# A mixture-of-experts router's work behind the dense products, and its second square behind the copy of its transposes

## The chip, the cores and the metric

The kernel runs on one core of a Trainium2 chip. The metric is the device time of one execution in microseconds (us); lower is better. The core has five engines with a list of instructions each: TensorE (PE), VectorE (DVE), ScalarE (ACT), GpSimd (POOL) and SyncE (SP, which issues most of the transfers).

## The reference

Two transformer blocks for 512 tokens of width 1024, all in float32. The first has two attention branches and a dense MLP, the second a gated linear attention, a pooling branch and a mixture of experts. The change lies between the second block's attention and its experts:

```python
x = x + merged @ w_out[l]
h2 = rmsnorm_2(x, norm2_g[l])
x = x + hier_moe(h2, w_router_group[l], b_router_group[l], w_router_expert[l], b_router_expert[l],
                 w_exp_gate[l], w_exp_up[l], w_exp_down[l])
```

`hier_moe` computes 4 group logits and 32 expert logits for each token, takes the best group, in it the two best experts, sorts the assignments by expert and runs each expert on its tokens:

```python
g_logits = (ht @ w_rg) + b_rg
g_p, g_idx = lax.top_k(jax.nn.softmax(g_logits, axis=-1), 1)
e_all = jnp.einsum('td,gde->tge', ht, w_re) + b_re
e_logits = e_all[jnp.arange(T), g_idx[:, 0]]
e_top, e_idx = lax.top_k(e_logits, TOP_K_IN_GROUP)
```

## The kernel before

The 512 tokens are four tiles (`t` = 0 to 3) of 128 tokens on 128 partitions. Float32 products are made from float32r operands split into a high and a low part, with three products each (`three`, recorded at L605 like every product of this kind).

The order of the work is not written out: a planner (`Plan`, L422) holds a list of streams, generators that yield one operation at a time. It gives an operation the earliest start that its model allows and emits the one with the least key; the second number of `plan.go` is the stream's rank:

```python
key = (s + 40.0 * st[0], st[1])
```

So a stream of rank 20 is set back by 800 model nanoseconds against rank 0. PSUM banks (eight) and memory are handed out in the order of the ranks as well. What comes out is a fixed list for each engine. Each engine takes its own list in order, and waits on semaphores where an instruction needs another engine's result.

Around the change:

- `rows_out` (L1343) is the projection with `w_out`. For its second half of columns a dense unit of 24 products of 128x512 is made for each tile, and `s_addx` adds the result to the residual `X[t]` (DVE, L1339), which frees the unit's PSUM bank. It runs in the main stream, of rank 6.
- `s_h2(t)` (L1844) takes the squares of both halves of `X[t]` (ACT, L1852), the reciprocal root of their mean (`rstd`, L727: after the sum at L1855 seven short DVE operations, L737 to L747), scales the row (ACT, L1860) and writes it to memory as `hd` (SP, L1861).
- `s_router(t)` (L1864) does, for each half `a` of the columns, four PE transposes of `X[t]` into a bank (L1895), an ACT copy as the high part (L1898), a DVE subtraction as the low part (L1899) and 8 small products with the router's weights (L605, outputs of 72x128 and 36x128, for the last tile 128x72 and 128x36). For tiles 0 to 2 an ACT copy (L1907) and a product (L1910) then fold and turn the sums. At last DVE makes the logits (L1924; for the last tile L1921 and L1922).
- `route` (L1940) chooses groups and experts for the tiles in three cuts, tiles 0 and 1 together, then 2, then 3 (L1976 to L1991 and L1931), ranks the tokens (L1931, L2072, with small products on PE) and reads the row numbers out of PSUM (L2089, L2090). 14 products follow on PE whose result nobody uses (`s_warm`).
- The first gather (POOL, L2219) needs the row numbers and the four `hd` writes. The expert stage starts with the transposes of the gathered rows (L2276). The stream of expert weights (SP, L685) pauses from the end of the projection until the first gather has landed (`seen`, L669).

Of the kernel before, what the change touches and what calls it, by code (L numbers as in the profile page):

```python
# [22 lines left out]
NT = 4  # L23
# [516 lines left out]
def fused(ctx: ExitStack, tc: tile.TileContext, x_in, wd, we, sm, cst, out):  # L540
# [19 lines left out]
    plan = Plan()  # L560
# [8 lines left out]
    def act(fn, n, r, w, k=1):  # L569
        return ("act", 0.833 * n + 115.0 * k, fn, tuple(r), tuple(w))  # L570

    def dve(fn, n, r, w, k=1, fast=False):
        return ("dve", (0.52 if fast else 1.04) * n + 70.0 * k, fn, tuple(r), tuple(w))
# [15 lines left out]
    def give(*bufs, toks=()):  # L589
        for b in bufs:  # L590
            b.last = max([b.last] + [k.last for k in toks])
            b.mem.give(b)
# [56 lines left out]
    rt = {}  # L649
# [646 lines left out]
    def gates(hT, res, n=4, att=False, rows=None):  # L1296
        hi, lo, toks = hT_cols(hT)
        for c in range(n):
            i = next(wi)
            wh, wl = yield from weight(i)  # L1300
            for u in range(2):
                ps, = yield take(banks=1)
                yield from cols_unit(ps, wh, wl, KD, 256, u * P, hi, lo, toks)
                b, = yield spare(KEEP_GATE if att else 0, 512)
                res.append(b)
                plan.go(s_gate(ps, b, rows), 2)
            done_weight(i)
# [87 lines left out]
    def new_parts():  # L1395

        b = yield taker(*[KD // NB * S] * (2 * NB))
        h, l = ([q for c in bs for q in carve(c, KD // NB)] for bs in (b[:NB], b[NB:]))
        return list(zip(h, l)) + [b]
# [86 lines left out]
    def s_alpha():  # L1486
        w = yield from load_small("alpha")
        h, l = yield from split(w.f, 256, [w], high=True)
        give(w)
        alpha.extend((h, l))  # L1490
# [283 lines left out]
    def pool_units(hT, rows):  # L1774
        hi, lo, toks = hT_cols(hT)
        for c in range(2):
            i = next(wi)
            wh, wl = yield from weight(i)
            for u in range(2):
                ps, = yield take(banks=1)  # L1780
                yield from cols_unit(ps, wh, wl, KD, 256, u * P, hi, lo, toks)
                plan.go(s_pool(2 * c + u, ps, rows), 2)
            done_weight(i)
# [12 lines left out]
    def block2_body(hT, rows, x4):  # L1796
        if "late" not in cgot:
            yield ("wait", lambda: "late" in cgot)
        plan.go(s_alpha(), 5)
        plan.go(s_par(["b_alpha_2", "gla_norm_g_2", "pool_scale", "pool_w"]), 5)  # L1800
        yield from token_major(hT, W2_CHUNKS, SECT2, True)
        yield from pool_units(hT, rows)
        gp, gg = [], []
        yield from gates(hT, gp, rows=rows)
        if len(pooled) < 4:
            yield ("wait", lambda: len(pooled) == 4)
        ptoks = [b for g in range(4) for b in pooled[g]]
        yield from branch2(lambda k: pooled[k][0].r, lambda k: pooled[k][1].r, ptoks, gp)
        give(*ptoks)
        yield from gates(hT, gg, rows=rows)  # L1810
        give(*hT[0], *hT[1], toks=hT[2])
        if OT.get("g") is None:
            yield ("wait", lambda: OT.get("g") is not None)
        mg = yield from new_parts()
        split_ahead[0] = AHEAD_OUT2
        yield from branch(OT["g"], ottok["g"], gg, gp, mg)
        give(rows[1], *(fac[t][0] for t in range(NT)), toks=rows[0])
        plan.go(s_par(["router", "b_router"]), 4)
        if "b_router" not in par:
            yield ("wait", lambda: "b_router" in par)  # L1820
        w = par["router"]
        wv = w.f.rearrange("p (k n) -> p k n", k=KD)
        yield dve(lambda: tt(wv, wv, gain("norm2_g_2")[:, :, None].to_broadcast([P, KD, 36]), ALU.mult), 288,
                  [w, par["gains"]], [w])
        wr, = yield taker(576, high=True)
        wrv, wrf = (q.rearrange("p (k z n) -> p k z n", k=KD, z=2) for q in (wr.r, wr.f))
        wr.need = 2
        yield act(lambda: A.activation(wrv[:, :, 0], wv, AF.Copy), 288, [w], [wr])
        yield dve(lambda: tt(wrv[:, :, 1], wv, wrf[:, :, 0], ALU.subtract), 288, [w], [wr])
        rt["w"] = wr  # L1830
        give(w)
        rt["x4"] = x4
        for t in range(NT):
            plan.go(s_router(t, x4[t]), 0)
        plan.go(route(), 0)
        yield from rows_out(mg, x4, True, EXP_AHEAD)

# [6 lines left out]
    def s_h2(t, xtok):  # L1844

        ss, = yield take(small=[2])
        ss.need = 2
        j, = yield take(512)
        for n in range(2):
            if xtok[n].t is None:  # L1850
                yield ("wait", lambda: xtok[n].t is not None)
            yield act(lambda: A.activation(j.f, X[t][:, n * 512:(n + 1) * 512], AF.Square, accum_out=ss.f[:, n:n + 1]), 512,  # L1852
                      [xtok[n]], [ss, j], k=2)
        give(j)
        yield dve(lambda: V.tensor_tensor(ss.f[:, 0:1], ss.f[:, 0:1], ss.f[:, 1:2], op=ALU.add), 1, [ss], [ss])  # L1855
        rb, r = yield from rstd(ss.f[:, 0:1], 1, D, ss)
        give(ss)
        rt["r", t] = rb, r
        h, = yield take(D)
        yield act(lambda: A.activation(h.f, X[t], AF.Copy, scale=r), D, [*xtok, rb], [h])  # L1860
        yield dma(lambda: SP.dma_start(hd[t * P:(t + 1) * P, :], h.f), 4 * P * D, [h], [hdt[t]])  # L1861
        give(h)

    def s_router(t, xtok):  # L1864
# [23 lines left out]
        for a in range(2):  # L1888
            if xtok[a].t is None:
                yield ("wait", lambda: xtok[a].t is not None)  # L1890
            ps, = yield take(banks=1)

            def f():
                for k in range(4):
                    T.transpose(ps.f[:, k * P:(k + 1) * P], X[t][:, (4 * a + k) * P:(4 * a + k + 1) * P], C["ident"])  # L1895

            yield pe(f, 4 * 56, [xtok[a], cgot["ident"][0]], [ps])
            yield act(lambda: A.activation(hs[a].r, ps.f, AF.Copy), 512, [ps], [hs[a]])  # L1898
            yield dve(lambda: V.tensor_tensor(ls[a].r, ps.f, hs[a].f, op=ALU.subtract), 512, [ps, hs[a]], [ls[a]])  # L1899
            give(ps)  # L1900
            hv, lv = (q[a].r.rearrange("p (k s) -> p k s", k=4) for q in (hs, ls))
            yield pe(lambda: products(a), 8 * (60 if t < NT - 1 else 108), [wr, hs[a], ls[a]], [po])
# [27 lines left out]
    def tt(o, a, b, op):  # L1930
        V.tensor_tensor(o, a, b, op=op)  # L1931
# [692 lines left out]
    def s_par(names, mem=None):  # L2624
        for n in names:
            par[n] = yield from load_small(n, mem)
# [117 lines left out]
```

## Time and profile before

| | us |
|---|---|
| median of 3 runs | 1342.98 |
| lowest, highest | 1341.76, 1343.89 |
| the profiled execution, its own time | 1340.58 |
| its span, first to last instruction | 1338.8 |
| PE busy | 1302.4 |
| DVE busy | 795.6 |
| ACT busy | 510.2 |

A row of the timeline gives the start, the duration, the engine, the line, the operation, output <- input with the tile's name, and in brackets how long the engine was idle before and what released it. Rows of equal instructions that follow each other are merged, with their count. The chain of waits is followed back from the last instruction. The granted clock of PE is given as a share of 2.4 GHz. Times are from the start of the span.

### The profile page before, as it was taken

To read this page: it belongs to the slowest core of one execution; us is meant where nothing else is said; L and a number is where in the kernel's file an instruction comes from. 1 tells how busy PE (TensorE), PEld (TensorE's weight loads), DVE (VectorE), ACT (ScalarE), POOL (GpSimd) and SP (SyncE) were. 2 spreads that over 40 slices of the span, in tenths; PEclk is the share of its full clock that TensorE was granted. 3 is DMA by queue.
4 is the path that set the end of the run, shared out by engine and by line. 5 is a ranking of instruction groups with operands and counts; after the bars stand their busy time and mean duration, and the time that the engine had idled before them with its cause. 6 is when DMAs were issued, how large, how long until landed. Compare 5 with 4: busy or idle time off the path is not lost.

```text
span 1338.8 us, 18461 instructions
## 1 busy us (share of the span) xinstructions
PE 1302.4 (97%) x6917; PEld 1003.8 (75%) x6917; DVE 795.6 (59%) x1912; ACT 510.2 (38%) x1084; POOL 22.1 (2%) x31
## 2 busy tenths in 40 slices
PE   6999999999999999999999999999999899999995
PEld 6998987778888888888888998888887544544543
DVE  7789988937454434334347448953374437555556
ACT  6663475643354313223225555542333211122212
POOL 0000000000000000000000000000000100000000
PEclk9999999999999999999999999999999899999998
DMA  6212220134132322222232221122262599999992
GB/s 245 95 64 95 75 85 32 41 132 143 35 112 94 111 95 94 94 95 94 95 112 87 90 85 64 63 73 100 95 241 94 201 407 408 409 408 407 408 368 79
DMA packets 59214, 205.11 MB, mean 153 GB/s; under 512 B 8435, under 2 KB 8947, under 8 KB 59123
## 3 DMA queue, kind: packets, MB, share of 16 engines
q1 hardware_dynamic: 56738, 199.72, 40.8%
q0 software_dynamic: 2384, 4.20, 0.9%
q8 instruction: 55, 0.90, 0.3%
q14 instruction: 37, 0.29, 0.1%
HBM read 204.15 MB, written 4.19 MB: 156 GB/s over the span
## 4 chain that ended last, share of the span: by engine, by line
PE 93%; DVE 3%; DMA 3%; ACT 1%; issue 1%; SPq 0%; DVEq 0%; ACTq 0%; POOLq 0%
PE bank L605 88%; DMA b<-in_we_dram 2%; PE bank L1231 1%; PE bank L2276 1%; PE bank L775 1%; DMA b<-in_wd_dram 1%; PE bank L1007 0%; DVE b L2560 0%; DMA b<-hd,b 0%; DVE b L1339 0%; PE bank L2336 0%; PE bank L1031 0%; PE bank L1895 0%; ACT b L2552 0%; DVE b L1931 0%
## 5 line engine op out<-in xcount | busy, mean ns | idle before, releaser
L605 PE MATMUL bank<-b,b 128*128 128x512 f32 (+9 forms) x6271 | 1250.1, 387 | 8.5 <-DVE b L1931 4.5
L605 PEld LDWEIGHTS bank<-b,b 128*128 128x128 f32 (+1 forms) x6271 | 937.0, 181 | 278.1 <-issue 102.4
L711 DVE TENSOR_TENSOR b<-b,b 128x1024 fp32r<-128x1024 f32 (+4 forms) x160 | 193.3, 1225 | 86.1 <-ACT b L710 83.2
L710 ACT ACTIVATE b<-b 128x1024 fp32r<-128x1024 f32 (+4 forms) x160 | 167.8, 1059 | 175.8 <-PE bank L605 165.7
L1339 DVE TENSOR_TENSOR b<-bank,b 128x512 f32<-128x512 f32 x176 | 111.2, 684 | 83.4 <-PE bank L605 82.7
L2293 ACT ACTIVATE b<-bank 128x256 f32<-128x256 f32 x16 | 6.2, 385 | 147.4 <-PE bank L605 141.1
L1404 DVE SCALAR_TENSOR_TENSOR b<-bank,b 128x512 f32<-128x512 f32 x32 | 22.1, 692 | 67.1 <-PE bank L605 65.4
L1407 ACT ACTIVATE b<-b 128x512 f32<-128x512 f32 x32 | 20.2, 632 | 96.2 <-DVE b L1404 96.2
L2296 DVE SCALAR_TENSOR_TENSOR b<-b,bank 128x256 f32<-128x256 f32 x16 | 6.7, 422 | 81.4 <-ACT b L2293 81.4
L2360 DVE SCALAR_TENSOR_TENSOR b<-bank,b,b 128x512 fp32r<-128x512 f32 x34 | 25.5, 751 | 28.9 <-ACT b L2359 28.9
L2359 ACT ACTIVATE b<-bank,b 128x512 fp32r<-128x512 f32 x34 | 23.4, 688 | 41.4 <-PE bank L605 38.8
L1208 ACT ACTIVATE b<-b,smalls 128x256 f32<-128x256 f32 (+3 forms) x64 | 32.6, 512 | 12.7 <-DVE smalls L1195 12.7
L1410 DVE TENSOR_TENSOR b<-b,b 128x512 fp32r<-128x512 f32 x32 | 22.1, 689 | 21.8 <-ACT b L1409 21.8
L1290 DVE TENSOR_TENSOR b<-bank,b 128x512 f32<-128x512 f32 x16 | 11.1, 692 | 36.7 <-PE bank L605 36.6
L1310 DVE SCALAR_TENSOR_TENSOR b<-b,bank 128x512 f32<-128x512 f32 x32 | 21.9, 684 | 15.2 <-PE bank L605 15.0
L775 PE MATMUL bank<-b,b 128*128 128x128 f32 x96 | 16.3, 303 | 12.9 <-DVE b L890 12.9
L1185 DVE CUSTOM_DVE_ANT_0 b<-bank,b 128x256 f32<-128x256 f32 (+3 forms) x64 | 26.2, 432 | 1.3 <-PE bank L605 1.2
L1139 DVE MATCH_REPLACE8 b<-smalls,b 128x256 f32<-128x256 f32 (+2 forms) x48 | 26.0, 550 | 0.0
L1291 ACT ACTIVATE b<-b 128x512 f32<-128x512 f32 x16 | 10.1, 630 | 40.5 <-DVE b L1290 40.5
L1138 DVE MAX8 smalls<-b 128x8 f32<-128x256 f32 (+2 forms) x48 | 25.4, 557 | 0.0
L794 ACT ACTIVATE b<-b 128x1024 f32<-128x1024 f32 x16 | 17.0, 1064 | 21.9 <-DVE b L1339 13.2
L2276 PEld LDWEIGHTS bank<-b,b 128*128 128x128 f32 (+1 forms) x136 | 14.9, 145 | 13.0 <-DVE b L2360 8.9
(207 smaller groups left out, 811.3 us busy)
## 6 DMA issues: line engine op xcount, KB each, us to landing
b<-in_we_dram SPq DMA_DIRECT2D x198, 512.0 KB
b<-in_wd_dram SPq DMA_DIRECT2D x138, 512.0 KB
b<-in_wd_dram SPq DMA_DIRECT2D x8, 516.0 KB
b<-in_x_dram SPq DMA_DIRECT2D x8, 512.0 KB
b<-in_wd_dram SPq DMA_DIRECT2D x6, 544.0 KB
b<-in_wd_dram SPq DMA_DIRECT2D x4, 536.0 KB
b<-in_wd_dram SPq DMA_DIRECT2D x4, 520.0 KB
hd<-b SPq DMA_DIRECT2D x4, 512.0 KB
```

Source lines behind the costliest of these rows:

```text
L605: T.matmul(o, l, r, start=start, stop=stop, skip_group_check=True)
L710: yield act(lambda: A.activation(h.r, b.f, AF.Copy), m, [b], [h])
L711: yield dve(lambda: V.tensor_tensor(l.r, b.f, h.f, op=ALU.subtract), m, [b, h], [l])
L775: T.transpose(banks[a].f[:, k * P:(k + 1) * P], x[:, (4 * a + k) * P:(4 * a + k + 1) * P], C["ident"])
L1138: yield dve(lambda: V.max(m8.f, acc.f), nk, [acc], [m8])
L1139: yield dve(lambda: V.match_replace(out=acc.f, in_to_replace=m8.f, in_values=acc.f, imm_value=GONE), nk, [m8, acc], [acc])
L1185: yield dve(lambda: V.tensor_tensor_reduce(out=p[h].f, in0=ps.f[:, i * nk:(i + 1) * nk], in1=mask, scale=1.0, scalar=GONE, op0=ALU.add, op ...
L1208: yield act(lambda: A.activation(ph, ph, AF.Exp, bias=ng_[:, h:h + 1], scale=0.125, accum_out=sm_[:, h:h + 1]), nk, [p[h], st], [p[h], st] ...
L1339: yield dve(lambda: V.tensor_tensor(X[t][:, a:a + w], ps.f[:, :w], X[t][:, a:a + w], op=ALU.add), w, [ps, before or xt[t]], [tok])
L2276: T.transpose(ps.f[:, k * P:k * P + n], g.f[0:n, (4 * a + k) * P:(4 * a + k + 1) * P], C["ident"][0:n, 0:n])
L2359: yield act(lambda: A.activation(yh.r[:, s], ps.f, AF.Copy, scale=gt), 512, [ps, sg], [yh], k=2)
L2360: yield dve(lambda: V.scalar_tensor_tensor(yl.r[:, s], ps.f, gt, yh.f[:, s], op0=ALU.mult, op1=ALU.subtract), 512, [ps, sg], [yl])
```

## The change

The router's streams of tiles 0, 1 and 2 are given rank 20 instead of 0; that of tile 3 and `route` stay at 0. In `s_h2` a tile's second square is yielded only once the copy of that tile's second transposes has been recorded (`("turned", t)`).

```diff
@@ -1831,7 +1831,7 @@
         give(w)
         rt["x4"] = x4
         for t in range(NT):
-            plan.go(s_router(t, x4[t]), 0)
+            plan.go(s_router(t, x4[t]), 0 if t == NT - 1 else 20)
         plan.go(route(), 0)
         yield from rows_out(mg, x4, True, EXP_AHEAD)
 
@@ -1849,6 +1849,8 @@
         for n in range(2):
             if xtok[n].t is None:
                 yield ("wait", lambda: xtok[n].t is not None)
+            if n and ("turned", t) not in rt:
+                yield ("wait", lambda: ("turned", t) in rt)
             yield act(lambda: A.activation(j.f, X[t][:, n * 512:(n + 1) * 512], AF.Square, accum_out=ss.f[:, n:n + 1]), 512,
                       [xtok[n]], [ss, j], k=2)
         give(j)
@@ -1896,6 +1898,8 @@
 
             yield pe(f, 4 * 56, [xtok[a], cgot["ident"][0]], [ps])
             yield act(lambda: A.activation(hs[a].r, ps.f, AF.Copy), 512, [ps], [hs[a]])
+            if a:
+                rt["turned", t] = True
             yield dve(lambda: V.tensor_tensor(ls[a].r, ps.f, hs[a].f, op=ALU.subtract), 512, [ps, hs[a]], [ls[a]])
             give(ps)
             hv, lv = (q[a].r.rearrange("p (k s) -> p k s", k=4) for q in (hs, ls))
```

What becomes of it in the lists. On PE, at the end of tile 1's second unit of the projection; in these rows `bank` is a PSUM bank, `b_3368` the residual `X`, `b_85` the identity. Before:

```order
L605 MATMUL bank_68<-b_8859,b_8619 128x512
L1910 MATMUL bank_69<-b_3890,b_9073 128x36
L1895 MATMUL bank_68<-b_85,b_3368 128x128 x4
L1895 MATMUL bank_69<-b_85,b_3368 128x128 x4
L605 MATMUL bank_66<-b_8918,b_8803 72x128
```

With the change, at the same place:

```order
L605 MATMUL bank_68<-b_8859,b_8619 128x512
L1897 MATMUL bank_66<-b_85,b_3368 128x128 x4
L605 MATMUL bank_68<-b_8780,b_8612 128x512
L605 MATMUL bank_68<-b_8781,b_8612 128x512
L605 MATMUL bank_68<-b_8780,b_8616 128x512
```

The folds, transposes and small products of the router (which go on after the last row of before) are gone from here; a set of transposes stands between this unit and the next, which writes the same bank.

On ACT, the stretch around and after tile 3's residual add; `b_3368` is `X`, `smalls` holds sums and roots, and the buffer that a copy writes tells the tile: before, `b_9074` is the high part of tile 2 and `b_9111` that of tile 3; with the change `b_8918` is that of tile 1, `b_9114` of tile 2, `b_9107` of tile 3. Before, from tile 1's scaled row on:

```order
L1860 ACTIVATE b_9136<-b_3368,smalls 128x1024
L1898 ACTIVATE b_9111<-bank_66 128x512
L1852 ACTIVATE b_8943,smalls<-b_3368 128x512
L1898 ACTIVATE b_9074<-bank_69 128x512
L1907 ACTIVATE b_9221<-bank_65 72x128
L1860 ACTIVATE b_9234<-b_3368,smalls 128x1024
L1852 ACTIVATE b_8992,smalls<-b_3368 128x512
L1898 ACTIVATE b_9111<-bank_69 128x512
L1860 ACTIVATE b_9308<-b_3368,smalls 128x1024
```

With the change, from tile 0's scaled row on:

```order
L1862 ACTIVATE b_9109<-b_3368,smalls 128x1024
L1900 ACTIVATE b_9107<-bank_68 128x512
L1911 ACTIVATE b_9138<-bank_69 72x128
L1900 ACTIVATE b_9107<-bank_69 128x512
L1854 ACTIVATE b_8966,smalls<-b_3368 128x512
L1862 ACTIVATE b_9187<-b_3368,smalls 128x1024
L1900 ACTIVATE b_8918<-bank_69 128x512
L1854 ACTIVATE b_8920,smalls<-b_3368 128x512
L1900 ACTIVATE b_9114<-bank_66 128x512
```

The square (now L1854) stands behind the copy (now L1900) in each tile; tile 3's square and scaled row stand ahead of tile 1's second copy.

On DVE with the change, from tile 3's logits (L1925, L1926) to tile 1's (L1928); `b_8919` and `b_9115` are the low parts of tiles 1 and 2:

```order
L1925 SCALAR_TENSOR_TENSOR b_8806<-bank_66,smalls,b_8785 128x36
L1926 SCALAR_TENSOR_TENSOR b_8806<-bank_66,smalls,b_8806 128x36
L1857 TENSOR_TENSOR smalls<-smalls 128x1
L737 TENSOR_SCALAR smalls<-smalls 128x1
L738 TENSOR_SCALAR smalls<-smalls 128x1
L740 TENSOR_SCALAR smalls<-smalls 128x1
L744 SCALAR_TENSOR_TENSOR smalls<-smalls 128x1
L745 SCALAR_TENSOR_TENSOR smalls<-smalls 128x1
L746 SCALAR_TENSOR_TENSOR smalls<-smalls 128x1
L747 SCALAR_TENSOR_TENSOR smalls<-smalls 128x1
L1903 TENSOR_TENSOR b_8919<-bank_69,b_8918 128x512
L1903 TENSOR_TENSOR b_9115<-bank_66,b_9114 128x512
```

Before, this root and both subtractions stood ahead of tile 3's residual add; now tile 1's root stands ahead of tile 1's second subtraction, and all of it behind tile 3's logits.

## Rows read from the trace of the kernel before

**Rows 1.** Page, part 1: busy us, share of the span, instructions of PE.
```profile
PE 1302.4 (97%) x6917; PEld 1003.8 (75%) x6917; DVE 795.6 (59%) x1912; ACT 510.2 (38%) x1084; POOL 22.1 (2%) x31
```

**Rows 2.** Timeline of DVE, 1000 to 1068 us: start, us, engine, line, operation, tiles.
```profile
1040.46 0.25 DVE L1924 SCALAR_TENSOR_TENSOR b<-bank,smalls,b 128x36 f32<-128x36 f32 x1
...
1042.81 0.19 DVE L1931 TENSOR_TENSOR b<-b 128x32 fp32r<-128x32 f32 x1
...
1044.52 0.69 DVE L1339 TENSOR_TENSOR b<-bank,b 128x512 f32<-128x512 f32 x1 [1.52 <-PE bank L605]
...
1045.12 0.41 DVE L1931 TENSOR_TENSOR b<-b 128x32 f32<-128x32 f32 x2
...
1045.96 0.42 DVE L1931 TENSOR_TENSOR b<-b,b 128x256 fp32r<-128x256 f32 x1
...
1046.30 0.15 DVE L1855 TENSOR_TENSOR smalls<-smalls 128x1 f32<-128x1 f32 x1
...
1046.59 0.69 DVE L1899 TENSOR_TENSOR b<-bank,b 128x512 fp32r<-128x512 f32 x1
...
1048.14 0.16 DVE L747 SCALAR_TENSOR_TENSOR smalls<-smalls 128x1 f32<-128x1 f32 x1
...
1049.54 0.16 DVE L1976 TENSOR_REDUCE b<-b 128x1 f32<-128x4 f32 x1
...
1053.90 0.17 DVE L2089 TENSOR_SCALAR b<-bank 128x16 int32<-128x16 f32 x1 [0.69 <-PE bank L605]
```

**Rows 3.** Chain of waits, 1000 to 1250 us: start, us, what.
```profile
1054.95 4.35 DMA b<-hd,b
```

**Rows 4.** Timeline of PE, 1000 to 1062 us.
```profile
1005.87 0.60 PE L1895 MATMUL bank<-b,b 128*128 128x128 f32 x4
...
1006.22 3.50 PE L605 MATMUL bank<-b,b 128*128 128x512 f32 x20
...
1024.17 0.31 PE L1910 MATMUL bank<-b,b 72*128 72x36 f32 x2
...
1025.12 1.09 PE L1895 MATMUL bank<-b,b 128*128 128x128 f32 x8 [0.64 <-DVE b L1339]
...
1027.62 2.66 PE L605 MATMUL bank<-b,b 128*36 128x128 f32 x21 [0.45 <-DVE b L1899]
...
1047.33 1.58 PE L605 MATMUL bank<-b,b 128*128 128x36 f32 x7 [0.38 <-DVE smalls L738]
...
1053.26 5.78 PE L605 MATMUL bank<-b,b 128*128 128x16 f32 x16 [1.03 <-DVE b L1931]
```

**Rows 5.** Chain of waits, 1235 us to the end.
```profile
1238.27 14.15 PE bank L605 x64
...
1295.37 10.38 DMA b<-in_we_dram
...
1305.75 1.28 issue
```

**Rows 6.** Timeline of ACT, 1000 to 1068 us.
```profile
1032.18 1.15 ACT L1860 ACTIVATE b<-b,smalls 128x1024 f32<-128x1024 f32 x1 [2.58 <-DMA hd<-b]
...
1045.24 0.63 ACT L1852 ACTIVATE b<-b 128x512 f32<-128x512 f32 x1 [3.71 <-DVE b L1339]
...
1045.96 0.60 ACT L1898 ACTIVATE b<-bank 128x512 fp32r<-128x512 f32 x1
```

**Rows 7.** Stretches: length, busy us (instructions) by engine, granted clock, DMA share, GB/s.
```profile
1040.00:1053.20 13.20, 7.77 (x37) 6.32 (x37) 9.60 (x48) 3.61 (x5) 1.31 (x2) 0.78 0.44 159
...
1048.00:1050.00 2.00, 0.92 (x5) 0.80 (x4) 1.17 (x8) 1.15 (x1) 0.00 (x0) 0.50 0.00 0
...
1057.00:1058.00 1.00, 1.00 (x5) 0.76 (x4) 0.00 (x0) 0.00 (x0) 0.40 (x1) 0.64 0.65 201
```

**Rows 8.** Timeline of PE, 1230 us to the end.
```profile
1299.37 5.82 PE L605 MATMUL bank<-b,b 128*128 128x512 f32 x24
```

**Rows 9.** Stretches, the end of the expert stage.
```profile
1240.00:1300.00 60.00, 60.00 (x292) 27.94 (x291) 30.94 (x54) 11.70 (x31) 1.93 (x2) 1.00 1.03 404
```

## The prediction

> **What bounds the kernel now.** I read the page first, then the chain of waits, then the timelines of TensorE (PE), VectorE (DVE) and ScalarE (ACT) over the router, then the end of the chain. PE is busy for 1302.4 of 1338.8 us [rows 1], so only its idle stretches can be won or lost. The largest is the router's end: the last dense product of the output projection is followed by tile 3's residual add at 1044.52, the row numbers leave PSUM at 1053.90 [rows 2], and the expert stage cannot begin before the first gathered rows land, at 1054.95 + 4.35 = 1059.30 [rows 3]. In between PE has little but 14 filler products, in the row of 16 at 1053.26 [rows 4]. So there are two quantities: when the dense block ends (call it T, the start of tile 3's add; now 1044.52), and how long the tail from T to the row numbers is (now 1053.90 - 1044.52 = 9.4 us). The tail is that short because, before T, the routers of tiles 0 to 2 are nearly through: of 8 sets of transposes 7, of 8 groups of small products 7, and all three folds stand ahead of it on PE.
>
> **The change, part by part.** In the planner the three router streams lose to any dense unit that is ready. The order shows what that makes: the four dense units follow each other, and five sets of transposes, seven groups of small products, all three folds and all of the ranking move behind T.
>
> *The dense block gets shorter.* I count from 1005.87, the first transposes [rows 4], up to which both orders are the same. Still ahead of T are:
> - 114 dense products. 64 of them take 14.15 us [rows 5], 0.221 each: 25.2 us.
> - 3 sets of transposes, each 1006.22 - 1005.87 = 0.35 [rows 4]: 1.1 us.
> - one group of 8 small products. The row of 21 at 1027.62 holds 15 of them and 6 dense ones in 2.66 us [rows 4]: (2.66 - 6 x 0.221) / 15 = 0.09 each, so 0.7 us.
> - a new wait. The dense units of the four tiles now all use one PSUM bank, so each waits until DVE has added the one before. Where PE waits for such an add today, 1025.12 - 1024.17 = 0.95 us pass [rows 4]. At three places a set of transposes covers 0.35 of it, at one the small products cover 0.7: 3 x 0.6 + 0.25 = 2.05 us.
>
> Together 29.1 us; with 0.2 until the add starts, T is at 1035.2, which is **9.4 us earlier**.
>
> *The tail gets longer.* It is now a chain through what has moved there, in the order of the three lists; each link waits for the one before:
> 1. Tile 3's add, then its first transposes in that bank: 0.69 [rows 2] and 0.05 hand-over, 0.75.
> 2. PE: transposes 0.35, three groups of small products 24 x 0.09 = 2.2, the fold of tile 0 0.31 [rows 4], and its logits 0.25 [rows 2], whose reading frees the bank for tile 3's second transposes: 3.2.
> 3. Those transposes 0.60 [rows 4], the ACT copy 0.60, and now the second square, 0.72 before the next ACT start [rows 6]: 1.9.
> 4. Tile 3's reciprocal root on DVE, eight short operations from 1046.30 to 1048.14 + 0.16, less the 0.60 that a low-part subtraction takes among them [rows 2]: 1.4.
> 5. ACT: the scaled row copy 1.15, which waited for that root, then tile 1's copy and square behind it: 1.15 + 0.60 + 0.72 = 2.5 [rows 6].
> 6. Tile 1's root, which stands ahead of its low-part subtraction on DVE: 1.4 + 0.69 [rows 2] = 2.1.
> 7. PE: 7 + 8 small products, transposes, tile 1's fold. Warm: 15 x 0.09 + 0.35 + 0.31 = 2.0. Seven small products took 1.58 us, 0.2 each, where the granted clock was falling to 0.50 [rows 4, 7], the 1.2 GHz level. In the tail PE has by then been mostly waiting for some 8 us, so I take 0.2 each and twice the rest: 4.2.
> 8. DVE: logits and choice for tiles 0 and 1 with tile 2's root in between. For one tile 1040.46 to 1042.81 + 0.19 = 2.5 [rows 2]; two tiles have two more operations (0.4) and the root's eight fill gaps and add about 0.8 (an estimate from these rows): 3.7.
> 9. Tile 2's subtraction 0.60, ranks 1.3 (from 1045.12 to the end of the row at 1045.96 [rows 2]), its fold and the sums 0.6: 2.5.
> 10. Tile 2's choice and ranks: 2.5 + 1.3 = 3.8.
> 11. Tile 3's choice and ranks: 1049.54 to 1053.90 [rows 2] = 4.4.
>
> Sum 30.5 us against 9.4: **21.1 us more**. The row numbers come 21.1 - 9.4 = 11.7 later, at about 1065.6. The four row writes to memory, the last behind tile 2's root in link 8, have landed by then; the gather and its 4.35 us are as before.
>
> Of link 7 the Trainium skill (TensorE: Matmul & The Clock Gate, "Back-to-back issue gap") says that cold products start N / 1.2 GHz apart, 107 ns for 128 columns. By it the 15 products cost 1.6 us instead of 3.0 and the sum is 1.4 less; the trace has 0.2 us each for narrower ones, and that I use.
>
> *The second square behind the copy.* Today tile 3's square stands ahead of its copy, 1045.24 against 1045.96 [rows 6]; that 0.72 leaves the way to the last products. In link 3 the same square stands before the root that tile 1 waits for, so it is in the sum once and buys nothing.
>
> *The weight stream.* One expert weight load more (seven instead of six) is issued before the stream pauses for the gather. At the end the last load lands at 1305.75 and PE goes on 1.28 later [rows 5], while PE's own products were through at 1299.37 + 5.82 = 1305.19 [rows 8]. A load takes 10.38 / 8 = 1.3 us with eight in flight [rows 5], so the stream ends up to 1.3 earlier relative to the gather, of which 1305.75 - 1305.19 = 0.56 can be used: **-0.6**.
>
> Net +11.1 us. Against the profiled execution (1340.58) that is 1351.7; the median of the three runs is 2.4 above it, and I add the sum to the median: **1354.1 us**, slower by 0.8%. Bounds: with link 7 warm, nothing lost in link 8 and 1 us of overlap in links 2 and 9, it is 4 less, +7; with the small products of link 2 and the ranks' matmuls at half clock too (15 x 0.11 and some 0.3 a tile), and no use of the load, +14.
>
> **The rivals.**
> - *The tail overlaps (faster).* The chains of the three tiles are independent; if the engines ran them side by side, DVE's own work would set the tail. 83 DVE operations stand in it; 48 took 9.60 us in the router's second half [rows 7], so 0.2 each and 16.6 us. The net is -9.4 + 16.6 - 9.4 - 0.6 = -2.8: 1340.2. It decides at a tail of 19.4 us. Against it: each engine takes its list in order, and links 5 and 6 put one tile's wait ahead of another's work on ACT and on DVE. 0.04.
> - *PE stays at half clock into the expert stage.* Now the clock is back within the filler products, at 0.64 in 1057 to 1058 [rows 7], some 4 us after they start. If after the longer quiet it came 4 us later, expert products would run at half speed for as long and lose 2.1: 1356.2. The Trainium skill (the same page, "HAM oscillation") says that after an idle gap TensorE is re-throttled and pays again on every restart, which would favour this; the same 14 products stand before the gather in both orders, which speaks against. 0.08.
> - *The weight stream alone sets the end.* Then the seventh load is worth its full 1.3 us: 1353.4. For it: the DMA share is 1.03 from 1240 to 1300; against: PE is busy for 60.00 of the same 60 us [rows 9]. 0.08.
> - *The planner's order is not what the diff says*: excluded, since the order shows the units together and the copies ahead of the squares.
>
> **How the numbers follow.** The forecast as worked out has 0.80; all cases but the first rival are slower, and their times lie inside its bounds. The range is 1342.98 + 7 to 1342.98 + 14, 1350 to 1357; outside it I leave about 0.2, the first rival among it. About 0.2%, 2.7 us, is what a measurement can tell from no change: the first rival is split between faster and the same, so faster 0.02, same 0.03, slower 0.95.
>
> **What would show it.** Right: tile 3's add near 1035, the row numbers near 1065, a tail of 28 to 32 us in which DVE waits for ACT squares and PE waits for DVE subtractions, the granted clock at 0.50 from some 5 us after the add until the filler products, and from the gather on the same expert stage, shifted. Each of the four dense units should be followed by a wait of some 0.6 us for the add. Wrong: a tail under 20 us, or a dense block that does not end 8 to 10 us earlier, or an expert stage whose length changes by more than 2 us.

## The result, and the profile after

The changed kernel takes 1354.59 us (median of 4 runs, 1352.7 to 1355.02) beside 1343.09 for the kernel before on the same chip (4 runs, 1341.76 to 1343.89): 11.5 us more, a ratio of 1.0091 with a 95% interval of 1.0078 to 1.0104. Its profiled run took 1355.02 us. Lines from L1852 of the kernel before on stand 2 later than there, those from L1899 on 4 later.

The timeline of PE over the router, of the kernel after, answers to [rows 4]:

```profile
1023.67 5.80 PE L605 MATMUL bank<-b,b 128*128 128x512 f32 x24 [0.34 <-DVE b L1339]
1029.31 0.60 PE L1897 MATMUL bank<-b,b 128*128 128x128 f32 x4
1030.26 5.79 PE L605 MATMUL bank<-b,b 128*128 128x512 f32 x24 [0.35 <-DVE b L1339]
1036.83 0.66 PE L1897 MATMUL bank<-b,b 128*128 128x128 f32 x4 [0.79 <-DVE b L1339]
...
1038.90 0.95 PE L605 MATMUL bank<-b,b 128*128 128x36 f32 x7 [0.32 <-DVE b L1903]
...
1048.39 1.91 PE L605 MATMUL bank<-b,b 128*36 128x128 f32 x15 [2.36 <-DVE b L1903]
1050.10 1.06 PE L1897 MATMUL bank<-b,b 128*128 128x128 f32 x4
...
1054.94 3.26 PE L605 MATMUL bank<-b,b 128*128 128x64 f32 x18 [3.51 <-DVE b L1935]
...
1066.30 5.77 PE L605 MATMUL bank<-b,b 128*128 128x16 f32 x16 [1.03 <-DVE b L1935]
1072.87 1.06 PE L2280 MATMUL bank<-b,b 128*128 128x128 f32 x8 [0.80 <-DMA b<-hd,b]
```

The dense units stand together, 6.59 us apart, each behind a wait for the add that frees its bank. Then PE mostly waits until the filler products in the row at 1066.30 and the expert stage at 1072.87, which began at 1059.44 before.

DVE in the same stretch, beside [rows 2]:

```profile
1036.09 0.69 DVE L1339 TENSOR_TENSOR b<-bank,b 128x512 f32<-128x512 f32 x1 [2.80 <-PE bank L605]
...
1040.13 0.26 DVE L1928 SCALAR_TENSOR_TENSOR b<-bank,smalls,b 128x36 f32<-128x36 f32 x1 [1.29 <-PE bank L1914]
...
1042.38 0.16 DVE L1857 TENSOR_TENSOR smalls<-smalls 128x1 f32<-128x1 f32 x1
...
1046.24 0.16 DVE L1857 TENSOR_TENSOR smalls<-smalls 128x1 f32<-128x1 f32 x1 [1.71 <-ACT b L1854]
...
1047.65 1.28 DVE L1903 TENSOR_TENSOR b<-bank,b 128x512 fp32r<-128x512 f32 x2
1051.47 0.25 DVE L1928 SCALAR_TENSOR_TENSOR b<-bank,smalls,b 128x36 f32<-128x36 f32 x1 [2.53 <-PE bank L1914]
...
1058.71 0.26 DVE L1928 SCALAR_TENSOR_TENSOR b<-bank,smalls,b 128x36 f32<-128x36 f32 x1 [1.59 <-PE bank L1914]
...
1062.58 0.15 DVE L1980 TENSOR_REDUCE b<-b 128x1 f32<-128x4 f32 x1
...
1066.93 0.17 DVE L2093 TENSOR_SCALAR b<-bank 128x16 int32<-128x16 f32 x1 [0.69 <-PE bank L605]
```

Tile 3's add (T) is at 1036.09 instead of 1044.52, the row numbers leave at 1066.93 instead of 1053.90, and the tail between the two is 30.84 us instead of 9.38. The traces start up to 1.2 us apart, so I compare them from the first of these eight adds, which stands at 1001.99 before and at 1001.61 here: aligned there, T is 1036.47, 8.05 earlier, and the row numbers come at 1067.31, 13.4 later. ACT shows link 5 of the prediction: the scaled row of tile 3, then the copy and the square of tile 1, for whose root DVE waits until 1046.24.

```profile
1043.97 1.15 ACT L1862 ACTIVATE b<-b,smalls 128x1024 f32<-128x1024 f32 x1 [1.62 <-DVE smalls L747]
1045.02 0.58 ACT L1900 ACTIVATE b<-bank 128x512 fp32r<-128x512 f32 x1
1045.50 0.62 ACT L1854 ACTIVATE b<-b 128x512 f32<-128x512 f32 x1
```

The stretches (length, busy time of each engine with instructions, granted clock, DMA share, GB/s) beside [rows 7]: half clock from about 1043.4 on (0.93 in the first row), 7 us after the add, and full clock again at about 1070.7 (0.64 in the third), 4.4 us after the row of the fillers begins.

```profile
1040.00:1044.00 4.00, 2.54 (x17) 2.07 (x16) 2.17 (x11) 1.24 (x4) 0.00 (x0) 0.93 0.04 17
1044.00:1070.00 26.00, 13.89 (x63) 11.70 (x62) 14.94 (x78) 6.96 (x13) 1.71 (x2) 0.50 0.17 63
1070.00:1071.00 1.00, 1.00 (x5) 0.76 (x4) 0.00 (x0) 0.00 (x0) 0.43 (x1) 0.64 0.58 139
1071.00:1072.00 1.00, 1.00 (x5) 0.54 (x3) 0.00 (x0) 0.00 (x0) 0.00 (x0) 1.00 0.78 262
```

The two profiled spans are 14.4 us apart (1353.2 and 1338.8), the medians 11.5. Between the profiles the granted clock of the expert stage differs too. Of the kernel before, a stretch in the middle of the stage and the last 24 expert products:

```profile
1143.00:1147.00 4.00, 4.00 (x17) 3.62 (x17) 2.05 (x7) 1.53 (x5) 0.99 (x1) 0.57 1.03 407
...
1307.00:1311.00 4.00, 3.97 (x20) 1.40 (x22) 0.24 (x1) 0.87 (x2) 0.00 (x0) 1.00 0.44 131
```

The same two places of the kernel after:

```profile
1156.00:1160.00 4.00, 4.00 (x28) 3.59 (x28) 2.73 (x8) 1.42 (x5) 0.99 (x1) 1.00 1.03 410
...
1319.00:1323.00 4.00, 3.31 (x9) 0.93 (x11) 0.49 (x1) 0.00 (x0) 0.00 (x0) 0.61 0.41 131
```

Before dropped to half clock in the middle and not at the end, the change the other way round. The last 24 expert products on PE, of before and then, with the 24 products ahead of them, of the change:

```profile
1307.03 5.37 PE L605 MATMUL bank<-b,b 128*64 128x512 f32 x24 [1.84 <-issue]
```

```profile
1311.89 5.85 PE L605 MATMUL bank<-b,b 128*128 128x512 f32 x24
1319.69 7.07 PE L605 MATMUL bank<-b,b 128*64 128x512 f32 x24 [1.95 <-issue]
```

The drop at the end is 1.7 us of the difference between the two spans (7.07 against 5.37). The drop in the middle cost PE 1.5 us on the spot, but traces without it do not reach the last 24 products sooner: from the first transposes of the expert stage to these products turned_alone needs 247.49 us and rank_7 247.69, where before needs 247.59; there PE waits longer ahead of them, 3.41 and 2.95 us instead of 1.84. Of the other four traces with that drop three have 247.6 to 247.7 and one, rank_alone, 248.24.

### The profile page after: what moved, and what is told of

The parts are those of the page before. It is cut to its first block, busy times and chain, and to the rows that moved or that the text cites. A ratio compares the mean times of both kernels' runs of the same rounds, so it can differ in the third digit from the quotient of the medians.

```text
span 1353.2 us, 18475 instructions
## 1 busy us (share of the span) xinstructions
PE 1307.8 (97%) x6917; PEld 1006.3 (74%) x6917; DVE 795.3 (59%) x1912; ACT 509.3 (38%) x1084; POOL 22.0 (2%) x31
## 5 line engine op out<-in xcount | busy, mean ns | idle before, releaser
L605 PE MATMUL bank<-b,b 128*128 128x512 f32 (+10 forms) x6271 | 1253.7, 388 | 17.2 <-DVE b L1935 9.5
L605 PEld LDWEIGHTS bank<-b,b 128*128 128x128 f32 (+2 forms) x6271 | 939.3, 181 | 289.3 <-issue 106.0
L2280 PEld LDWEIGHTS bank<-b,b 128*128 128x128 f32 (+1 forms) x136 | 14.3, 140 | 13.4 <-DVE b L2364 8.9
```

The source lines that it names most:

```text
L605: T.matmul(o, l, r, start=start, stop=stop, skip_group_check=True)
```

## The experiments

The theory: the loss is the tail less the shorter dense block, one for one. The tail is long because three tiles' work goes through in-order lists of PE, ACT and DVE with one tile's wait ahead of another's work. Rivals: the "turned" wait makes the loss; the low clock does; the weight loads ahead of the pause set the end. In every run the kernel before ran beside it on the same chip. T, tail and row numbers are from each run's trace, moved so that the first residual add stands at 1001.99. The ratios are taken over all runs and differ a little from those of the medians.

| kernel | T | tail | row numbers | time, us | beside before | ratio, 95% interval |
|---|---|---|---|---|---|---|
| before | 1044.52 | 9.38 | 1053.90 | | | 1 |
| the change | 1036.47 | 30.84 | 1067.31 | 1354.59 | 1343.09 | 1.0091 [1.0078, 1.0104] |
| rank_alone | 1036.47 | 29.55 | 1066.02 | 1352.54 | 1340.84 | 1.0086 [1.0072, 1.0100] |
| turned_alone | 1044.20 | 9.22 | 1053.42 | 1341.81 | 1340.84 | 0.9999 [0.9986, 1.0011] |
| rank_7 | 1038.43 | 23.43 | 1061.86 | 1349.15 | 1340.84 | 1.0063 [1.0047, 1.0079] |
| h2_20_alone | 1045.05 | 9.46 | 1054.51 | 1341.17 | 1340.84 | 0.9998 [0.9988, 1.0008] |
| six_loads | 1036.47 | 31.02 | 1067.49 | 1354.73 | 1342.16 | 1.0093 [1.0078, 1.0109] |
| warm_tail | 1036.47 | 40.78 | 1077.25 | 1363.11 | 1342.16 | 1.0153 [1.0137, 1.0169] |
| two_choices | 1040.64 | 10.94 | 1051.58 | 1339.73 | 1342.16 | 0.9980 [0.9971, 0.9989] |
| choices_behind | 1036.47 | 26.92 | 1063.39 | 1350.20 | 1342.16 | 1.0061 [1.0047, 1.0075] |
| change_two_choices | 1033.23 | 31.15 | 1064.38 | 1352.07 | 1342.37 | 1.0077 [1.0063, 1.0091] |
| choices_at_once | 1033.23 | 25.37 | 1058.60 | 1345.96 | 1342.37 | 1.0035 [1.0023, 1.0047] |
| two_choices_loads | 1040.67 | 10.94 | 1051.61 | 1336.79 | 1342.37 | 0.9966 [0.9954, 0.9978] |
| before_loads | 1044.48 | 8.82 | 1053.30 | 1340.14 | 1341.15 | 0.9987 [0.9977, 0.9997] |

**Which part of the change: rank_alone and turned_alone.** Against the change:

```
 rank_alone, in s_h2:
-            if n and ("turned", t) not in rt:
-                yield ("wait", lambda: ("turned", t) in rt)
 turned_alone, in block2_body:
-            plan.go(s_router(t, x4[t]), 0 if t == NT - 1 else 20)
+            plan.go(s_router(t, x4[t]), 0)
```

Expected of rank_alone:

> The change with the rank 20 kept and the wait of the second squares taken out. Theory: all of the loss comes from the rank, which gathers the four dense units and leaves the three tiles' streams behind tile 3's add (L1339); that add stands at 1036 as in the change. Without the wait the second squares, and with them the roots of tiles 1 and 2, stand before the end of the dense block, where ACT and DVE have room, so links 5 and 6 of the tail (2.3 + 2.15 us in the trace of the change) shrink to about a low-part subtraction and PE's own work: the tail is 27 to 29 us instead of 30.8 and the time 1351 to 1353. Rival A, the step as the prediction has it (the wait buys nothing and costs nothing): 1354 to 1355, a tail of 30 to 31. Rival B, the wait helps behind the rank: over 1355.5.

Expected of turned_alone:

> The wait of the second squares kept, all four streams at rank 0 as before. Theory: the order of the dense units is as before, tile 3's add stands at 1043 to 1045 and the row numbers 8.5 to 9.5 us behind it; copying before squaring takes 0.72 us off the way to the last small products, but the root then ends later and the logits wait for it, so the time is that of before within 1 us, 1342 to 1344. Rival A, the copy ahead of the square is on the path that sets the end: 0.5 to 1 us faster. Rival B, the wait also costs something by itself: 1345 or more.

The rank alone gives the loss (1.0086); the wait alone gives nothing (0.9999), as its T and tail are those of before. Behind the rank the wait makes the tail 1.3 us longer in the traces (30.84 against 29.55), which the times, with overlapping intervals, cannot tell from nothing. I had expected a tail of 27 to 29. What held it up is in the timeline of PE of rank_alone:

```profile
1049.32 3.26 PE L605 MATMUL bank<-b,b 128*128 128x64 f32 x18 [3.08 <-DVE b L1935]
1052.43 1.11 PE L1897 MATMUL bank<-b,b 128*128 128x128 f32 x4
```

The group of 18 begins with the rank products of tiles 0 and 1, for which PE waits 3.08 us. Tile 2's second transposes stand behind them in the list, start at 1052.43, and tile 2's logits come at 1057.06 only.

**How much rank: rank_7.** Against rank_alone:

```
-            plan.go(s_router(t, x4[t]), 0 if t == NT - 1 else 20)
+            plan.go(s_router(t, x4[t]), 0 if t == NT - 1 else 7)
```

> Rank 7 in the place of 20 and no wait of the second squares. Theory: what counts is how much of the three streams' work lies before tile 3's add. With rank 7 the planner lets more of it in between the dense units, so the add comes later than in the change (1037 to 1039) and the tail is shorter, 19 to 24 us; the row numbers come at 1057 to 1060 and the time is 1346 to 1349. Rival, the gain of the gathered dense block and the cost of the tail do not go together (the tail stays at 28 us or more once the streams rank behind at all): 1351 or more.

As the theory has it for T and tail (1038.43 and 23.43). The row numbers came at 1061.86 and the median is 1349.15, over the range in both, the first by 1.9 us: less rank, less loss.

**Only the squares and roots late: h2_20_alone.** Against before, in s_router:

```
-        plan.go(s_h2(t, xtok), 0)
+        plan.go(s_h2(t, xtok), 0 if t == NT - 1 else 20)
```

> The kernel before, but for the squares, roots and scaled rows of tiles 0 to 2, which get rank 20 while the transposes, copies and small products keep rank 0. Theory: work of these three tiles that the logits alone wait for can be late without a longer tail, as long as PE's part of it is not: tile 3's add comes 0 to 1.5 us earlier, the tail stays at 8 to 10 us, the time is 1341 to 1343.5. Rival, the roots come late and the choices of tiles 0 to 2 slide behind tile 3's add: a tail of 11 us or more and 1344 or more.

T, tail and time are those of before (0.9998). But the rank made squares and scaled rows up to 2 us later and hardly the roots, for which the logits wait: the last operation of tile 2's root, before and then in h2_20_alone:

```profile
1040.18 0.16 DVE L747 SCALAR_TENSOR_TENSOR smalls<-smalls 128x1 f32<-128x1 f32 x1
```

```profile
1040.29 0.16 DVE L747 SCALAR_TENSOR_TENSOR smalls<-smalls 128x1 f32<-128x1 f32 x1
```

Those of tiles 0 and 1 come less than 0.6 us later. So the run shows that this rank on squares and scaled rows alone costs no time. That roots may be late, and that it is the part that PE shares (the transposes and small products) that may not, is not shown by it.

**The seventh load: six_loads.** Against the change, in s_wload:

```
-                if PAUSE and "x4" in rt and "paused" not in rt and rt["x4"][NT - 1][1].t is not None:
+                if PAUSE and "x4" in rt and "paused" not in rt and u >= 178:
```

> The change, but the stream of expert weights pauses for the gather after as many loads as before (six behind the first thirteen's block counted as in the prediction, 178 of the whole program instead of 179). Theory, the step of the seventh load: from the first load after the pause to the issue of the last one the stream takes 236.0 to 236.3 us with 180 loads (before, and three of the runs above) and 234.4 with 179 (the change). With one load more to do, the last expert's weights land about 0.9 us later than PE can use them: PE's wait before the last 24 products rises from 1.95 to about 2.8, and the time is 0.5 to 1 us more than the change, 1354.5 to 1356 beside a before of 1343. Rival, the load is not used: the wait stays at 1.95 and the time is that of the change within 0.3.

The rival holds here: 1.0093 against 1.0091, and in the trace PE waits no longer than in the change before the last 24 products.

```profile
1319.24 5.37 PE L605 MATMUL bank<-b,b 128*64 128x512 f32 x24 [1.74 <-issue]
```

**The low clock: warm_tail.** Against the change, in s_router between the low part and the small products:

```
+FILL = {(3, 1): 4, (1, 1): 9, (2, 1): 9}
...
             give(ps)
+            n = FILL.get((t, a), 0)
+            if n:
+                fb, = yield take(banks=1)
+                for _ in range(n):
+                    yield pe(lambda: mm(fb.f, CR["ones"], hs[a].r[:, 0:512], True, True), mmcost(512), [hs[a], cgot["late"][1]], [fb])
+                give(fb)
```

> The change with 22 products of ones added on PE in the tail (4 before tile 3's second small products, 9 before tile 1's, 9 before tile 2's), into a bank that nobody reads; the output is the same. Theory: the tail is a chain over ACT, DVE and PE, and PE's own work on it is small (the 15 small products, transposes and folds of link 7 and the ranks' products, some 5 us at half clock), so with the clock kept at 1.00 it can get at most 2 us shorter, and the added products delay what stands behind them by some tenths where they run at half clock: a tail of 29 to 31.5 us, time within 1.5 us of the change. Rival, the low clock is what makes the tail long: a tail of 27 us or less and 1351 or less.

Both expectations missed: the tail is 9.9 us longer and the time 1.0153 of before. PE of warm_tail (one line more ahead, so that the adds are L1340 and the low parts L1904):

```profile
1042.69 3.60 PE L606 MATMUL bank<-b,b 128*128 128x512 f32 x12 [1.41 <-DVE b L1904]
...
1050.76 5.37 PE L606 MATMUL bank<-b,b 128*128 128x512 f32 x25 [2.67 <-DVE b L1904]
...
1060.37 7.34 PE L606 MATMUL bank<-b,b 128*128 128x64 f32 x27 [3.65 <-DVE b L1942]
```

The fillers were to run while the small products waited for the low part. Those of tiles 3 and 1 got the bank that this same subtraction reads (its transposes' bank, just given back), and so waited for it too. The nine of tile 2 got another bank, but stand behind the first rank products of tiles 0 and 1, for which PE waits 3.65 us. So all 22 stood in the chain: 9.9 / 22 = 0.45 us each, twice the 0.22 of full clock. So this run does not tell what a full clock in the tail would be worth; that stays open. It shows what products in a chain cost there.

**Banks and portions of the choice: two_choices and change_two_choices.** The first against before, the second against the change, at L170:

```
-ROUTE_CUTS = (0, 2), (2, 3), (3, 4)
+ROUTE_CUTS = ((0, 3), (3, 4))
```

Expected of two_choices:

> The kernel before (all streams at rank 0, no wait of the second squares), but the choices are made in two portions instead of three: tiles 0 to 2, then tile 3 (ROUTE_CUTS 0-3, 3-4). That takes one bank less from the time at which the routing stream starts, and one serial portion of choice and ranks less. Theory: the routing stream's banks are what the dense units of the second column half lack; with one more of them tile 3's add comes 2 to 4 us earlier than 1044.5 and the tail stays at 9 to 10 us; the gather and the resumed weight loads come 2 to 3.5 us earlier and so does the end: 1339 to 1341.5 beside a before of 1343. Rival, the stream of weights sets the end: PE waits over 3 us before the last 24 products and the time is that of before within 1 us.

Expected of change_two_choices:

> The change, with the choices in two portions (tiles 0 to 2, then tile 3) as in two_choices. Theory: the routing stream takes one bank less, so the dense units of the second column half no longer wait for the add that frees their only bank, a wait of 0.95 us behind each of them in the trace of the change (6.6 us apart for 24 products of 5.65): tile 3's add comes 2 to 3.5 us before 1036.09. In the tail one portion of choice and ranks goes (3.9 to 4.35 us in the change), but tiles 0 and 1 must wait for tile 2, so no more than 1 to 3 us is gained there: row numbers at 1061 to 1064, time 1349 to 1352. Rival, the dense block is bound by PE and the bank's wait would be spent anyway: the add at 1035.5 or later and 1352.5 or more.

Two_choices is faster than before, 0.9980 [0.9971, 0.9989]. Up to T its PE shows no wait at all, where before has four, of 0.64, 0.69, 0.45 and 0.18 us; T is 3.9 earlier and the tail 1.6 longer. The edit gives back a bank and takes away a portion at once; this run does not part the two. DVE of two_choices:

```profile
1040.64 0.69 DVE L1339 TENSOR_TENSOR b<-bank,b 128x512 f32<-128x512 f32 x1 [0.18 <-PE bank L605]
...
1051.58 0.17 DVE L2093 TENSOR_SCALAR b<-bank 128x16 int32<-128x16 f32 x1 [0.68 <-PE bank L605]
```

In change_two_choices the order of PE's list has the dense units alternate between bank_68 and bank_69, where the change has bank_68 alone, and they run through without a wait, 24 products in 5.50 us (adds at 1022.00, 1027.50 and 1033.00):

```profile
1010.67 22.29 PE L605 MATMUL bank<-b,b 128*128 128x512 f32 x96 [0.35 <-DVE b L1339]
```

T comes 3.24 us before that of the change, as expected. The last three adds were 6.58 apart in the change; two sets of transposes (0.35 each) and eight small products (0.7) have moved behind T, so 3.24 - 1.4 = 1.8 us of this belong to the shared bank, at three of the four units: waits of 0.6, 0.6 and 0.25 us, and units that take 5.50 us unbroken instead of 5.64 behind a wait. The tail, 31.15, is not shorter, against what I expected of one portion less; the time, 1352.07, is at the edge of the range.

**The order of the tail: choices_behind and choices_at_once.** Choices_behind against rank_alone, and choices_at_once against choices_behind:

```
 choices_behind, in block2_body:
-        plan.go(route(), 0)
+        plan.go(route(), 20)
 choices_at_once, at L170:
-ROUTE_CUTS = (0, 2), (2, 3), (3, 4)
+ROUTE_CUTS = ((0, 4),)
```

Expected of choices_behind:

> The rank 20 kept, no wait of the second squares (as in rank_alone), and the routing stream with the choices also at rank 20, so that on PE tile 2's second transposes stand ahead of the rank products of tiles 0 and 1 and not behind them. Theory: in rank_alone PE waited 3.08 us for DVE with the rank products at the head of its list while tile 2's transposes, ready for 4 us, stood behind them; put ahead, tiles 1 and 2 go side by side, tile 2's logits come at 1049 to 1052 instead of 1057.06, the choices follow each other without a wait, and the tail is 24 to 27 us instead of 29.55: 1348 to 1350.5. Rival, the portions of the choice set the tail whatever stands ahead: 29 us or more and no gain over rank_alone.

Expected of choices_at_once:

> As choices_behind (rank 20 for the three streams and the routing stream, no wait of the second squares), but with one portion of choices for all four tiles. Theory: in choices_behind the logits of all tiles were there 14.5 us after tile 3's add, and three portions of choice and ranks then took 12.4 us one after the other; one portion for four tiles takes 5 to 6.5 us (two tiles took 4.8 in rank_alone, 1046.57 to 1051.4). So the tail is 20 to 22.5 us instead of 26.92, the two banks that are no longer held bring tile 3's add to 1032 to 1034, and the time is 1341 to 1345: the rank's loss is then nearly gone. Rival, the tail is set by the streams at half clock and not by the portions: 25 us or more and 1347 or more.

With tile 2's transposes ahead of the rank products the logits of tiles 1 and 2 come 0.6 us apart, the later at 1049.55 of its trace, the tail is 26.92 and the time 1350.20, all as the theory had it. DVE of choices_behind:

```profile
1035.27 0.69 DVE L1339 TENSOR_TENSOR b<-bank,b 128x512 f32<-128x512 f32 x1 [3.00 <-PE bank L605]
...
1049.55 0.26 DVE L1928 SCALAR_TENSOR_TENSOR b<-bank,smalls,b 128x36 f32<-128x36 f32 x1 [0.18 <-PE bank L1914]
...
1062.19 0.17 DVE L2093 TENSOR_SCALAR b<-bank 128x16 int32<-128x16 f32 x1 [0.79 <-PE bank L605]
```

One portion instead of three brings T to 1033.23 and the row numbers to 1058.60, but the single portion, from 1049.21 to 1058.02 of its trace, takes 8.8 us where I had allowed 5 to 6.5. So the tail (25.37) is in the range of the rival (25 or more) and the time (1345.96) between the two. Of the rank's loss 0.35% is left. The portion on DVE, from its first operation to the row numbers:

```profile
1049.21 0.17 DVE L1980 TENSOR_REDUCE b<-b 128x4 f32<-128x16 f32 x1
...
1058.02 0.17 DVE L2093 TENSOR_SCALAR b<-bank 128x16 int32<-128x16 f32 x1 [2.07 <-PE bank L605]
```

**Loads ahead of the pause: two_choices_loads and before_loads.** Against two_choices and against before, in s_wload:

```
-                if PAUSE and "x4" in rt and "paused" not in rt and rt["x4"][NT - 1][1].t is not None:
+                late = "x4" in rt and rt["x4"][NT - 1][1].t is not None
+                rt["late"] = rt.get("late", 0) + late
+                if PAUSE and "paused" not in rt and rt["late"] > 2:
```

Expected of two_choices_loads:

> two_choices with two weight loads more before the pause (180 instead of 178 in the whole program). Theory after six_loads: the stream ends 246 us after it resumes and PE's expert stage needs as long, so loads ahead of the pause buy nothing that can be measured: within 0.15% of two_choices (ratio 0.9965 to 0.9995). Rival, PE waits for the last weights in the runs in which its clock does not drop on the way (2.95 and 3.41 us of waiting in the traces of rank_7 and turned_alone, against 1.95): 0.7 to 1.5 us faster than two_choices, a ratio of 0.997 or less.

Expected of before_loads:

> The kernel before with two weight loads more ahead of the pause (180 instead of 178) and nothing else. It separates two readings: two_choices_loads stood at 0.9966 of before and two_choices at 0.998, six_loads at 1.0093 against 1.0091 for the change. Theory A: loads ahead of the pause shorten the end, because the stream (246 us from its resumption to the last landing) then runs out earlier than PE; then this kernel is 1 to 2.5 us faster than before, a ratio of 0.9980 to 0.9993, and PE waits 1.7 to 1.95 us before the last 24 products. Theory B: the loads buy nothing, the gap between the two kernels is chance of the clock drops in the expert stage; ratio 0.9993 to 1.0010.

Two_choices_loads, 0.9966, lies in both ranges and is the fastest kernel of the study, 0.34% under before. Before_loads, 0.9987 [0.9977, 0.9997], speaks for theory A: 1.7 us by the ratio, of which 0.6 may be row numbers that come earlier. The row numbers of two_choices_loads come as those of two_choices. From the expert stage's first transposes to its last 24 products the traces of these two, with 180 loads ahead of the pause, show 245.65 and 245.84 us (PE starting at 1057.20 and 1058.35), all others 246.6 to 248.2 (246.82 in the change, 247.59 before). The last 24 products of two_choices_loads, then of before_loads, where the clock dropped:

```profile
1302.85 5.37 PE L605 MATMUL bank<-b,b 128*64 128x512 f32 x24 [1.74 <-issue]
```

```profile
1304.19 7.07 PE L605 MATMUL bank<-b,b 128*64 128x512 f32 x24 [1.94 <-issue]
```

## Why the prediction was right, and where a step was not

Forecast 1354.1 (1350 to 1357), measured 1354.59; slower, as forecast. By its steps:

- **The dense block**: T was forecast at 1035.2; aligned it is 1036.47, 1.3 later. The term mis-sized is the dense product: 0.221 us, the price in the expert stage [rows 5]. The wait for the bank is as forecast: from a set of transposes to the next unit 0.95 us pass (1029.31 to 1030.26), 0.35 and 0.6. But the 24 products of a unit behind such a wait take 1029.31 - 1023.67 = 5.64 us, 0.235 each (unbroken, in change_two_choices, 5.50, 0.229 each), and 96 x 0.014 = 1.3. Of the five sets and seven groups that the prediction has moving behind T, one each stood there before. Added up again, three of its figures are 0.1 off (T comes 9.3 earlier, link 2 is 3.1, link 7 4.3), which changes nothing.
- **The tail**: 30.5 forecast, 30.84 measured. Link by link, forecast and then measured between the rows above: 0.75, 0.74; 3.2, 3.61; 1.9, 1.94; 1.4, 1.6; 2.5, 2.3; 2.1, 2.15; 4.2, 3.1; 3.7, 3.5; 2.5, 3.8; 3.8, 3.9; 4.4, 4.35. Three are off by 0.4 or more and nearly cancel. Link 2 is 0.4 short: for 0.32 of it PE waits for a low part (1038.90). Link 7 is 1.1 too long: the 15 small products took 1050.10 - 1048.39 = 1.71 us at half clock, 0.11 each and not the 0.2 of the row of seven at 1047.33 [rows 4], which is of another shape. By the formula of the Trainium skill (TensorE: Matmul & The Clock Gate, "Back-to-back issue gap"), N / 1.2 GHz cold, 128 columns take 107 ns and the 15 an estimated 1.6 us; the trace agrees. Link 9 is 1.3 too short: the row of 18 at 1054.94 holds, with the rank products, tile 2's last eight small products, for which the sum has no term, and all run at half clock (3.26 us), which I had priced in the upper bound alone.
- **The second square buys nothing**: right. turned_alone stands at 0.9999, and behind the rank it costs 1.3 us of tail, inside the noise of the times.
- **The seventh load, -0.6**: not shown. The 0.77 us by which the expert stage of the change is shorter (from 1072.87 to 1319.69, 246.82, against 1059.44 to 1307.03, 247.59) cannot be put down to the load: six_loads, without it, has 246.58. Nor does the clock drop of before explain it, since turned_alone and rank_7 need as long without the drop. Taking the load away changed nothing that can be measured (six_loads), while two loads more on the kernel before gained 0.13%. What one load is worth stays open, below some 3 us either way.
- **The row numbers set the end**: borne out over the runs. Aligned they come 13.4 us later in the change, 12.1 in rank_alone, 9.5 in choices_behind, 8.0 in rank_7, 4.7 in choices_at_once and 2.3 earlier in two_choices; the times differ by 11.5, 11.7, 8.0, 8.3, 3.6 and -2.4. Of large shifts up to 2 us do not arrive at the end. They are not alone: in two_choices_loads they come 2.3 earlier, as in two_choices, but the time is 5.6 less, so what the loads ahead of the pause give comes on top. The forecast missed the shift by 1.7 (11.7 against 13.4) and the median by 0.5, so what is given back after the gather hid an error, and that the median came so close is partly luck; in the profiled pair what is given back is not seen, since the clock drop at the end adds 1.7 us to the change's span.
- **The rivals**: a tail that overlaps (decided at 19.4 us) did not come, for the reason given against it. PE's lists in order are shown to cost 2.6 us by choices_behind (29.55 to 26.92), but even the best tail behind rank 20 was 25.37. Half clock into the expert stage did not come either: full clock was back 4.4 us after the row of the fillers begins, before 4.5 (0.64 in 1057 to 1058 [rows 7]). The Trainium skill's rule that TensorE pays again on every restart (same page, "HAM oscillation") holds in the tail, at half clock for 26 us; it did not reach past the fillers. That the weight stream alone sets the end is not borne out for the change: there the last load was issued at 1307.15 and took 9.9 us, to 1317.05, while PE's products ahead of the last 24 ran until 1311.89 + 5.85 = 1317.74, and without the seventh load the time is the same (six_loads). In before the load lands last, 0.56 us after PE's products, and two loads more ahead of the pause gained 0.13%.

## What to carry to other kernels

Putting independent work behind a dense block pays only if that work overlaps as well afterwards; here it lengthened the dense block by 8 us and the tail, once alone there, by 21.5, since in-order lists make one tile's wait another's. Before giving such work a lower rank, write down the chain that is left behind the last dense product and price it link by link, each product at the clock that the rows show for a mostly waiting PE. Look at what a stream holds while it waits: one PSUM bank and one portion of choices less for the routing stream took PE's waits out of the dense block and, with two weight loads more ahead of the pause, gave the version that beats both kernels (1336.79 beside 1342.37).

## What the runs showed of the hardware that was not expected

PE's granted clock fell to 0.50 for 3 to 4 us, the 1.2 GHz level, in the middle of the expert stage while PE was busy for the whole of it, with no idle time ahead: 17 instructions in 4.00 us of before against 28 in the same place of the change, in the rows above. It came at one place of the program, in 5 of the 14 traces (before, rank_alone, h2_20_alone, two_choices, choices_behind), and cost PE about 1.5 us: before needs 50.5 us from 1110.53 to 1161.05 for what takes the change 49.0 from 1124.14 to 1173.16. Ahead of the last 24 products, where PE waits anyway, nothing of it is left in four of the five (the result section has the lengths). A second place is the last 24 expert products, behind a wait of 1.9 to 3.4 us: half clock in 7 of the 14, 6.82 to 8.24 us instead of 5.37, the longest in turned_alone:

```profile
1305.54 8.24 PE L605 MATMUL bank<-b,b 128*64 128x512 f32 x24 [3.41 <-issue]
```

It did not come in rank_alone after 1.95 or in rank_7 after 2.95 us of waiting, and four traces have neither drop. That such drops make up much of the 3 to 7 us by which runs of one kernel differ is likely: the mean granted clock of each run is on record, and of the 23 runs of before beside rank_alone the nine at 0.993 or 0.994 took 1339.1 to 1340.5 us, the six at 0.989 or 0.990 1341.7 to 1345.8. It is not shown, since the runs without a profile do not tell where their clock was low. What decides on a drop stays open.
